# A state space recurrence in two levels, and cache pages requested in two of three units

## The chip, the cores and the metric

The kernel runs on one core of a Trainium2 chip. The metric is the device time of one execution in microseconds, as the median of several runs. Five engines work side by side, each on its own queue in program order: TensorE (PE, with its weight loads as PEld), VectorE (DVE), ScalarE (ACT), GpSimd (POOL), and SyncE (SP), which here only issues DMA transfers.

## The reference

One layer of a hybrid decoder for 512 prompt tokens and 8 x 4 sample tokens (544 columns). The normalized input goes through one wide projection and then into three branches: causal pooling, sparse attention over a paged cache, and a complex diagonal state space. Each is gated, projected and merged, and one output projection follows. Two pieces matter here:

```python
# compression: each block of 64 cached tokens is projected to one key and one value
kc = jnp.einsum('bnlkd,lde->bnke', blk[:, :, :, 0] + pe_cmp[0][:, None, :], w_phi[0])
vc = jnp.einsum('bnlkd,lde->bnke', blk[:, :, :, 1] + pe_cmp[1][:, None, :], w_phi[1])
# state space: h[s] = a * h[s-1] + bu[s], complex, for 64 groups x 64 states
_, _, hr, hi = lax.associative_scan(_complex_affine_combine, (a_re, a_im, bu_re, bu_im), axis=1)
```

## The kernel before

**Units.** The weights lie in blocks of 128 x 1024 (`wd`), one per unit. `M_LIST` gives the order of the projection's output tiles, `UNITS` one entry per weight block, and the loop at the end of `tile_hybrid_kernel` walks through them with `step`. In `in_unit` a unit is one half of the columns (272) of one output tile over all 16 blocks of rows. Every product is done three times by `mm3` (L149 to L151), with a high and a low half of each operand, so a unit has 48 matmuls of 272 columns. A pool unit (`pool_unit`) has 24. Units take the PSUM tiles `d` (three buffers) in turn.

**A step.** `step` writes out by hand what is queued for a unit: deferred functions (mostly stores, put off with `later` by one step), one `next` for each background generator in `bg`, the evacuation of the unit before (`pend_evac`), the split of the weights two units ahead (`w_split`: ScalarE rounds to `whi`, L144, and `lo_eng[0]` subtracts to get `wlo`, L145), the next weight load (`w_load`, L133, three raw buffers, so it waits until a split has freed one), and then the unit's matmuls. With `early[0]` set, the split and the load stand ahead of the generators. All loads and stores are issued on SP, in this order.

**The background.** `main_bg` runs beside the projection: `g_compress`, `g_ssm`, `g_compress_prompt`, `g_prompt`, `g_decode` one after the other; each `yield` ends its share of a step. `g_params` runs beside `g_compress` and prepares the constants of the state space on VectorE (L690 and following), from an input `par` that it loads itself.

**Compression.** `g_compress` has 16 jobs (8 sequences x 2 halves), each with 16 pages of 128 KB in a tile `ca` (two buffers), and takes three units for a job: 5, 5 and 6 of the 16 steps of d, two matmuls each (L620). Each matmul reads all 16 pages. In each of the three units `fetch` asks for a part of the next job's pages: SP reads the page numbers (L583) and issues one DMA per page (L587).

**State space.** `g_ssm` works on chunks of 8 tokens: 64 chunks for the prompt. Matmuls give the contribution of each chunk to the state at its end, copied to `SH` [128, 2 (real, imaginary), 32, 73]: columns 0 to 7 are the samples' states, 8 is zero, 9 to 72 the 64 chunks. The recurrence then goes over the chunks one after the other (L885 to L897): SH[c+1] += A8 * SH[c], complex, as four VectorE operations on [128, 2, 32] (two products, their sum, the addition), six chunks per step. `A8` is the coefficient of 8 tokens. While it runs, `lo_eng[0]` is GpSimd, so that L145 leaves VectorE. Then come the sample states (L904 to L907), the store of them and of the last prompt state (`hp`), two steps' ends, and the outputs: tiles `T` and `bd` are cleared by GpSimd, `make_u` (L935 to L941) builds factors on VectorE and GpSimd, and the first matmuls of the next step (L1006) read them. The pools `wk_s`, `rk_s` and `yk_s` follow each other in the same memory; `sq` lives through `g_ssm`.

Of the kernel before, what the change touches and what calls it, by code (L numbers as in the profile page):

```python
# [10 lines left out]
F32 = mybir.dt.float32  # L11
# [3 lines left out]
OP = mybir.AluOpType  # L15
# [51 lines left out]
def kernel(ctx, tc, a):  # L67
    nc = tc.nc
    pe, dve, act, pool, sp = nc.tensor, nc.vector, nc.scalar, nc.gpsimd, nc.sync
# [5 lines left out]
    def R(name, bufs=1):  # L75
        return tc.tile_pool(name=name, bufs=bufs, side="right")
# [9 lines left out]
    def bank(tag, bufs):  # L86
        return psb.tile([128, 512], F32, name=tag, tag=tag, bufs=bufs)
# [33 lines left out]
    lo_eng = [dve]  # L121
# [33 lines left out]
    def later(fn):  # L155
        deferred.append(fn)
# [425 lines left out]
    def gather(dsts, table, col):  # L582
        _, regs = nc.values_load_multi_w_load_instructions(  # L583
            PT[0:1, col:col + len(dsts)], engines=[mybir.EngineType.SP], min_val=0, max_val=NPOOL - 1,
            skip_runtime_bounds_check_because="the page table is clamped on the chip after its load")
        for dst, r in zip(dsts, regs):
            sp.dma_start(dst, a[table].rearrange("(g p) x -> g p x", p=128)[bass.ds(r, 1)]  # L587
                         .rearrange("g p x -> (g p) x"))

    def g_compress():  # L590
        with ExitStack() as s:
            cp = s.enter_context(R("cmp"))
            wphi = cp.tile([128, 2, 32, 64], F32, name="wphi")
            sp.dma_start(wphi, a["wphi"])
            ca_s = ExitStack()
            cap = ca_s.enter_context(R("ca", 2))
            jobs = [(b, h) for b in range(8) for h in range(2)]
            tiles = {}

            def fetch(n, pages):  # L600
                if n >= len(jobs):
                    return
                b, h = jobs[n]
                if n not in tiles:
                    tiles[n] = cap.tile([128, 16, 256], F32, name="ca")
                gather([tiles[n][:, pg, :] for pg in pages], f"c{h}", b * 16 + pages[0])
            for pg in range(0, 16, 4):
                fetch(0, range(pg, pg + 4))
                yield
            acc_b = None  # L610
            for n, (b, h) in enumerate(jobs):
                t = tiles.pop(n).rearrange("q g (k e j) -> q g k e j", k=2, j=8)
                if h == 0:
                    acc_b = bank("s", 2)
                for d0, d1, pgs in ((0, 5, (0, 6)), (5, 10, (6, 11)), (10, 16, (11, 16))):
                    fetch(n + 1, range(*pgs))
                    for d in range(d0, d1):
                        dd = h * 16 + d
                        for k in range(2):
                            pe.matmul(acc_b[k * 64:(k + 1) * 64, :128], lhsT=wphi[:, k, dd, :],  # L620
                                      rhs=t[:, :, k, d, :], start=(dd == 0), stop=(dd == 31))
                    yield
                if h:
                    act.activation(KC[:, b, :], acc_b[:, :128], AF.Copy)
            yield
            ca_s.close()
        done.add("cache")
# [171 lines left out]
    def g_ssm():  # L799
        while not {("su", 7), "params"} <= done:  # L800
            yield
        AR, BB, CC, A8 = (SSM[n] for n in ("AR", "BB", "CC", "A8"))
        s = ExitStack()
        sq = s.enter_context(R("ssm"))
        SH = sq.tile([128, 2, 32, 73], F32, name="sh")
# [42 lines left out]
        for n in range(10):  # L848
            i = n - 2
# [5 lines left out]
            i = n - 1  # L855
# [26 lines left out]
        rk_s = ExitStack()  # L882
        rp = rk_s.enter_context(R("ssmr", 2))
        m = dve.tensor_tensor
        lo_eng[0] = pool  # L885
        for c0 in range(0, 64, 6):
            for c in range(c0, min(64, c0 + 6)):
                prev = SH[:, :, :, 8 + c]
                nxt = SH[:, :, :, 9 + c]
                t1_ = rp.tile([128, 2, 32], F32, name="t1")  # L890
                t2_ = rp.tile([128, 2, 32], F32, name="t2")
                m(t1_, A8[:, 0], prev, op=OP.mult)  # L892
                m(t2_, A8[:, 1], prev[:, ::-1], op=OP.mult)  # L893
                m(t1_, t1_, t2_, op=OP.add)  # L894
                m(nxt, nxt, t1_, op=OP.add)  # L895
            yield
        lo_eng[0] = dve  # L897
        t1_ = rp.tile([128, 2, 32, 8], F32, name="h41", bufs=1)
        t2_ = rp.tile([128, 2, 32, 8], F32, name="h42", bufs=1)
        h0v = SH[:, :, :, 0:8]  # L900
# [5 lines left out]
            m(t1_[:, r_], t1_[:, r_], t2_[:, r_], op=OP.subtract if r_ == 0 else OP.add)  # L906
        m(S2, S2, t1_, op=OP.add)  # L907
        later(lambda: sp.dma_start(a["ssms"], S2))
        hp = rp.tile([128, 2, 32], F32, name="hp", bufs=1)
        pool.tensor_copy(hp, SH[:, :, :, 72])  # L910
        later(lambda: sp.dma_start(a["ssmp"], hp))
        yield
        yield
        rk_s.close()
        yk_s = ExitStack()
# [55 lines left out]
        for n in range(11):  # L971
            i = n - 3
# [11 lines left out]
            i = n - 2  # L984
# [8 lines left out]
            i = n - 1  # L993
# [6 lines left out]
            i = n  # L1000
# [623 lines left out]
    def main_bg():  # L1624
        yield from g_compress()
        early[0] = True
        yield from g_ssm()
        early[0] = False
        yield from g_compress_prompt()
        yield from g_prompt()  # L1630
        yield from g_decode()
        early[0] = True
        att_s.close()
        open_y()
        yield from prep_y(0, ypool, "pz")
        yield from prep_z()
# [4 lines left out]
    for u in range(4, len(UNITS)):  # L1641
# [6 lines left out]
        if un[0] == "in":  # L1648
            kind, i = M_LIST[un[1]]
# [166 lines left out]
    for u in range(first_tail, len(UNITS)):  # L1816
# [9 lines left out]
        else:  # L1826
# [4 lines left out]
            m, half = un[1:] if un[1] < 14 else ((14, 0), (15, 0), (14, 1), (15, 1))[u - len(UNITS) + 4]  # L1831
# [174 lines left out]
```

## Time and profile before

| | |
|---|---|
| median of 3 runs | 2327.85 us (2323.11 to 2331.73) |
| the profiled execution | 2324.99 us, span 2323.2 us |
| TensorE busy | 2243.1 us (97%), 19478 matmuls |
| TensorE weight loads busy | 2150.7 us (93%) |
| VectorE busy | 1110.6 us (48%) |
| ScalarE, GpSimd busy | 653.3 us (28%), 163.9 us (7%) |
| mean DMA rate | 154 GB/s |
| mean granted TensorE clock | 0.986 |

Times in the rows are microseconds from the start of the span. A busy TensorE is not TensorE at its peak, since matmuls are pipelined; so its waits and the number of matmuls in a stretch say more than its busy share. [...] The compression runs from about 75 to 451 us, the recurrence from 547 to 639.

### The profile page before, as it was taken

Reading aid. Unit: us, or ns where it says so; the run is one execution under the profiler, and the core shown is the slowest. Engines: PE = TensorE matmul, PEld = TensorE weight load, DVE = VectorE, ACT = ScalarE, POOL = GpSimd, SP = SyncE. Lnnn points to the kernel's source line nnn. Section 1 sums busy time; section 2 is a strip of 40 time slices with the busy share of each in tenths; the row PEclk is TensorE's granted clock in tenths of the full one; section 3 lists DMA queues with packets and bytes.
Section 4 is the critical chain, followed back from the end, with each engine's and each line's share of the span. In section 5 each row is a group of like instructions: output and inputs, shape, how many; then the busy total and the mean of one; then the engine's idle time right before and its main releaser. Section 6 shows DMA issues by size and latency. Waiting matters only on the chain.

```text
span 2323.2 us, 47074 instructions
## 1 busy us (share of the span) xinstructions
PE 2243.1 (97%) x19478; PEld 2150.7 (93%) x19478; DVE 1110.6 (48%) x2157; ACT 653.3 (28%) x1113; POOL 163.9 (7%) x132
## 2 busy tenths in 40 slices
PE   8999899999899999999999999999999999999995
PEld 8988799998889999999999998789999999999995
DVE  6234552256963246666665343323444536453225
ACT  5111111131022114444444222222332222222231
POOL 2000000142261000000000000000000002100003
PEclk9999999999999999999999999999999999999998
DMA  6766667562245655233222668875543645343333
GB/s 233 207 177 159 169 193 203 148 141 82 80 129 140 208 188 173 84 96 116 90 85 74 185 197 253 273 255 162 158 131 129 209 157 199 133 136 102 116 99 97
DMA packets 297128, 358.25 MB, mean 154 GB/s; under 512 B 137169, under 2 KB 219730, under 8 KB 296530
## 3 DMA queue, kind: packets, MB, share of 16 engines
q1 hardware_dynamic: 296914, 355.23, 50.3%
q8 instruction: 154, 2.52, 0.4%
q14 instruction: 60, 0.49, 0.1%
HBM read 309.33 MB, written 54.13 MB: 156 GB/s over the span
## 4 chain that ended last, share of the span: by engine, by line
PE 78%; DVE 5%; SPq 1%; DMA 1%; issue 1%; POOL 0%; ACT 0%; DVEq 0%; POOLq 0%; ACTq 0%
PE d L149 23%; PE d L151 22%; PE d L150 22%; PE o L1234 2%; PE s L1170 2%; PE t L1210 2%; PE s L620 1%; DVE t L892 1%; SPq L587 1%; DVE t L893 1%; DVE t L894 1%; PE s L953 1%; DVE sh L895 1%; PE o L1514 1%; PE s L1431 1%
## 5 line engine op out<-in xcount | busy, mean ns | idle before, releaser
L149 PE MATMUL d<-xh,whi 128*128 128x272 f32 x3424 | 1012.6, 296 | 20.5 <-DVE e L324 14.4
L151 PE MATMUL d<-xl,whi 128*128 128x272 f32 x3424 | 989.6, 289 | 0.0
L150 PE MATMUL d<-xh,wlo 128*128 128x272 f32 x3424 | 988.8, 289 | 0.0
L149 PEld LDWEIGHTS d<-xh,whi 128*128 128x128 f32 x3424 | 650.3, 190 | 47.4 <-issue 30.9
L151 PEld LDWEIGHTS d<-xl,whi 128*128 128x128 f32 x3424 | 649.8, 190 | 0.8 <-DVE xl L232 0.6
L150 PEld LDWEIGHTS d<-xh,wlo 128*128 128x128 f32 x3424 | 650.4, 190 | 0.0
L145 DVE TENSOR_TENSOR wlo<-wr,whi 128x1024 fp32r<-128x1024 f32 x298 | 378.1, 1270 | 300.8 <-ACT whi L144 298.3
L144 ACT ACTIVATE whi<-wr 128x1024 fp32r<-128x1024 f32 x309 | 323.0, 1052 | 474.9 <-PE d L151 376.4
L324 DVE TENSOR_TENSOR e<-d,rstd 128x272 f32<-128x272 f32 x186 | 81.7, 439 | 410.7 <-PE d L151 397.6
L149 PE MATMUL d<-mh,whi 128*128 128x272 f32 x512 | 148.4, 290 | 0.0
L151 PE MATMUL d<-ylA,whi 128*128 128x272 f32 x512 | 147.6, 288 | 0.0
L149 PE MATMUL d<-yhA,whi 128*128 128x272 f32 x512 | 147.5, 288 | 0.0
L150 PE MATMUL d<-yhA,wlo 128*128 128x272 f32 x512 | 147.4, 288 | 0.0
L151 PE MATMUL d<-ml,whi 128*128 128x272 f32 x512 | 147.4, 288 | 0.0
L150 PE MATMUL d<-mh,wlo 128*128 128x272 f32 x512 | 147.1, 287 | 0.0
L151 PE MATMUL d<-ylB,whi 128*128 128x272 f32 (+2 forms) x384 | 110.8, 289 | 0.0
L150 PE MATMUL d<-yhB,wlo 128*128 128x272 f32 (+2 forms) x384 | 110.8, 288 | 0.0
L149 PE MATMUL d<-yhB,whi 128*128 128x272 f32 (+2 forms) x384 | 110.6, 288 | 0.0
L149 PEld LDWEIGHTS d<-mh,whi 128*128 128x128 f32 x512 | 96.4, 188 | 0.0
L151 PEld LDWEIGHTS d<-ylA,whi 128*128 128x128 f32 x512 | 96.4, 188 | 0.0
L150 PEld LDWEIGHTS d<-yhA,wlo 128*128 128x128 f32 x512 | 96.3, 188 | 0.0
L151 PEld LDWEIGHTS d<-ml,whi 128*128 128x128 f32 x512 | 96.3, 188 | 0.0
(386 smaller groups left out, 2528.4 us busy)
## 6 DMA issues: line engine op xcount, KB each, us to landing
wr<-wd SPq DMA_DIRECT2D x309, 512.0 KB, 3.9
ca<-c SPq DMA_DIRECT2D x256, 128.0 KB, 3.3
gk<-ck SPq DMA_DIRECT2D x128, 128.0 KB, 2.2
gv<-cv SPq DMA_DIRECT2D x128, 128.0 KB, 3.3
gates<-e SPq DMA_DIRECT2D x48, 272.0 KB, 4.4
lg<-gates SPq DMA_DIRECT2D x48, 272.0 KB, 4.0
xo<-xT SPq DMA_DIRECT2D x32, 136.0 KB, 3.5
yT<-yo SPq DMA_DIRECT2D x32, 136.0 KB, 1.8
```

Of the source, the lines that this page charges most:

```text
L144: act.activation(hi, r, AF.Copy)
L145: lo_eng[0].tensor_tensor(lo, r, hi.bitcast(F32), op=OP.subtract)
L149: pe.matmul(ps, lhsT=h, rhs=xh, start=start, stop=False)
L150: pe.matmul(ps, lhsT=l, rhs=xh, start=False, stop=False)
L151: pe.matmul(ps, lhsT=h, rhs=xl, start=False, stop=stop)
L324: dve.tensor_tensor(out[:, cols(hf)], ps[:, :HALF], rstd[:, cols(hf)], op=OP.mult)
L587: sp.dma_start(dst, a[table].rearrange("(g p) x -> g p x", p=128)[bass.ds(r, 1)] .rearrange("g p x -> (g p) x"))
L620: pe.matmul(acc_b[k * 64:(k + 1) * 64, :128], lhsT=wphi[:, k, dd, :], rhs=t[:, :, k, d, :], start=(dd == 0), stop=(dd == 31))
L892: m(t1_, A8[:, 0], prev, op=OP.mult)
L1170: pe.matmul(st[n][k][:, off:off + nk], lhsT=QS[pg][k][:, qt * 128:(qt + 1) * 128], rhs=KS[br, k][j][:, :nk], start=(j == 0), stop=(j == 1))
L1210: pe.transpose(b[:, c:c + 128], st[n][k][:, c:c + 128], ident)
L1234: pe.matmul(o[hs[k], qt * 128:(qt + 1) * 128], lhsT=VN[:, kb, br, pg // 4, hs[k]], rhs=st[n][k][:, off + kb * 128:off + (kb + 1) * 128], s ...
```

## The change

Compression: the 16 pages of the next job are asked for in the first two of its three units, eight in each; none in the third. Recurrence: the 64 chunks become 8 blocks (k) of 8 chunks (j). First the powers 1 to 8 of the coefficient are made (`PP`, and `PS_` with the sign for the imaginary part). Then all blocks advance together over their own chunks (seven advances of 8 columns), the last chunks of the blocks advance one after the other (seven of one column), and each chunk j of blocks 1 to 7 gets the end of the block before, times the power j + 1 (seven of 7 columns). An advance has four operations as before. The columns lie 8 elements apart in `SH`. `lo_eng[0]` stays VectorE. `hp` moves from the pool `rp` to `sq`. The number of steps between the first step of the recurrence and the one that clears `T` stays 13.

```diff
--- before.py
+++ after.py
@@ -612,8 +612,9 @@
                 t = tiles.pop(n).rearrange("q g (k e j) -> q g k e j", k=2, j=8)
                 if h == 0:
                     acc_b = bank("s", 2)
-                for d0, d1, pgs in ((0, 5, (0, 6)), (5, 10, (6, 11)), (10, 16, (11, 16))):
-                    fetch(n + 1, range(*pgs))
+                for d0, d1, pgs in ((0, 5, (0, 8)), (5, 10, (8, 16)), (10, 16, ())):
+                    if pgs:
+                        fetch(n + 1, range(*pgs))
                     for d in range(d0, d1):
                         dd = h * 16 + d
                         for k in range(2):
@@ -882,19 +883,48 @@
         rk_s = ExitStack()
         rp = rk_s.enter_context(R("ssmr", 2))
         m = dve.tensor_tensor
-        lo_eng[0] = pool
-        for c0 in range(0, 64, 6):
-            for c in range(c0, min(64, c0 + 6)):
-                prev = SH[:, :, :, 8 + c]
-                nxt = SH[:, :, :, 9 + c]
-                t1_ = rp.tile([128, 2, 32], F32, name="t1")
-                t2_ = rp.tile([128, 2, 32], F32, name="t2")
-                m(t1_, A8[:, 0], prev, op=OP.mult)
-                m(t2_, A8[:, 1], prev[:, ::-1], op=OP.mult)
-                m(t1_, t1_, t2_, op=OP.add)
-                m(nxt, nxt, t1_, op=OP.add)
-            yield
-        lo_eng[0] = dve
+        PP = rp.tile([128, 2, 32, 8], F32, name="pp8", bufs=1)
+        PS_ = rp.tile([128, 2, 32, 8], F32, name="ps8", bufs=1)
+
+        def tmps(n):
+            return [rp.tile([128, 2, 32, 8], F32, name=f"t{i}")[:, :, :, :n] for i in (1, 2)]
+
+        dve.tensor_copy(PP[:, 0, :, 0], A8[:, 0, 0])
+        dve.tensor_copy(PP[:, 1, :, 0], A8[:, 1, 1])
+        for n in (1, 2, 4):
+            xr_, xi_ = PP[:, 0, :, 0:n], PP[:, 1, :, 0:n]
+            wr_, wi_ = (PP[:, r_, :, n - 1:n].to_broadcast([128, 32, n]) for r_ in range(2))
+            t1_, t2_ = tmps(n)
+            m(t1_[:, 0], xr_, wr_, op=OP.mult)
+            m(t1_[:, 1], xi_, wi_, op=OP.mult)
+            m(t2_[:, 0], xr_, wi_, op=OP.mult)
+            m(t2_[:, 1], xi_, wr_, op=OP.mult)
+            m(PP[:, 0, :, n:2 * n], t1_[:, 0], t1_[:, 1], op=OP.subtract)
+            m(PP[:, 1, :, n:2 * n], t2_[:, 0], t2_[:, 1], op=OP.add)
+        dve.tensor_scalar(PS_[:, 0], PP[:, 1], -1.0, None, op0=OP.mult)
+        dve.tensor_copy(PS_[:, 1], PP[:, 1])
+        yield
+        V = SH[:, :, :, 9:73].rearrange("q r g (k j) -> q r g k j", j=8)
+
+        def advance(dst, src, e, n):
+            t1_, t2_ = tmps(n)
+            m(t1_, PP[:, 0:1, :, e:e + 1].to_broadcast([128, 2, 32, n]), src, op=OP.mult)
+            m(t2_, PS_[:, :, :, e:e + 1].to_broadcast([128, 2, 32, n]), src[:, ::-1], op=OP.mult)
+            m(t1_, t1_, t2_, op=OP.add)
+            m(dst, dst, t1_, op=OP.add)
+
+        for j in range(1, 8):
+            advance(V[:, :, :, :, j], V[:, :, :, :, j - 1], 0, 8)
+            if j in (1, 3, 4, 6, 7):
+                yield
+        for k in range(1, 8):
+            advance(V[:, :, :, k:k + 1, 7], V[:, :, :, k - 1:k, 7], 7, 1)
+            if k in (4, 7):
+                yield
+        for j in range(7):
+            advance(V[:, :, :, 1:8, j], V[:, :, :, 0:7, 7], j, 7)
+            if j in (1, 3, 5, 6):
+                yield
         t1_ = rp.tile([128, 2, 32, 8], F32, name="h41", bufs=1)
         t2_ = rp.tile([128, 2, 32, 8], F32, name="h42", bufs=1)
         h0v = SH[:, :, :, 0:8]
@@ -906,10 +936,9 @@
             m(t1_[:, r_], t1_[:, r_], t2_[:, r_], op=OP.subtract if r_ == 0 else OP.add)
         m(S2, S2, t1_, op=OP.add)
         later(lambda: sp.dma_start(a["ssms"], S2))
-        hp = rp.tile([128, 2, 32], F32, name="hp", bufs=1)
+        hp = sq.tile([128, 2, 32], F32, name="hp")
         pool.tensor_copy(hp, SH[:, :, :, 72])
         later(lambda: sp.dma_start(a["ssmp"], hp))
-        yield
         yield
         rk_s.close()
         yk_s = ExitStack()
```

## Rows read from the trace of the kernel before

**Rows 1.** The chain that ended last, by engine (the page, part 4)

```profile
PE 78%; DVE 5%; SPq 1%; DMA 1%; issue 1%; POOL 0%; ACT 0%; DVEq 0%; POOLq 0%; ACTq 0%
```

**Rows 2.** TensorE's waits, 140 to 345 us: us in total, times, longest

```profile
PE s L620 <- DMA ca<-c: 21.7, 6, 7.2
```

**Rows 3.** Stretches: length, engines' busy time (instructions), clock, DMA share, GB/s

```profile
...
283.10:290.20 7.10, 0.00 (x0) 0.00 (x0) 1.73 (x2) 1.06 (x1) 0.00 (x0) 0.78 0.59 142
314.90:317.20 2.30, 0.00 (x0) 0.00 (x0) 2.09 (x8) 1.26 (x2) 0.00 (x0) 1.00 0.73 188
sum 21.20, PE 0.00 PEld 0.00 DVE 11.11 ACT 3.37 POOL 0.00; mean PE 0.00 PEld 0.00 DVE 1.85 ACT 0.56 POOL 0.00
```

**Rows 4.** The same view, stretches of 10 us; first in each, PE

```profile
170.00:180.00 10.00, 10.00 (x79) 9.35 (x75) 1.22 (x4) 0.00 (x0) 0.00 (x0) 0.78 0.68 228
...
320.00:330.00 10.00, 10.00 (x86) 9.68 (x85) 7.51 (x36) 0.00 (x0) 0.00 (x0) 0.94 0.41 81
...
550.00:560.00 10.00, 10.00 (x83) 10.00 (x81) 9.41 (x27) 1.35 (x2) 3.41 (x2) 1.00 0.27 83
```

**Rows 5.** The same view, the recurrence and an undisturbed part of the compression

```profile
546.90:657.73 110.83, 91.59 (x680) 90.15 (x678) 102.79 (x288) 15.84 (x16) 35.63 (x20) 0.93 0.27 88
350.00:450.00 100.00, 100.00 (x927) 95.63 (x928) 20.61 (x28) 17.30 (x22) 0.00 (x0) 1.00 0.62 181
```

**Rows 6.** SP in order of time: start, us, line, transfer, count

```profile
271.33 2.40 SPq L587 DMA_DIRECT2D ca<-c  x5
...
282.42 2.42 SPq L587 DMA_DIRECT2D ca<-c  x5
...
316.32 7.20 SPq L395 DMA_DIRECT2D gsc<-e  x12
```

**Rows 7.** VectorE in order of time; in brackets idle before, releaser

```profile
304.13 0.18 DVE L690 TENSOR_SCALAR v<-par 128x32 f32<-128x32 f32 x1 [18.70 <-DMA par<-spar]
...
307.45 0.43 DVE L324 TENSOR_TENSOR e<-d,rstd 128x272 f32<-128x272 f32 x1
...
309.55 1.22 DVE L145 TENSOR_TENSOR wlo<-wr,whi 128x1024 fp32r<-128x1024 f32 x1 [0.51 <-ACT whi L144]
```

**Rows 8.** Transfers issued from 150 to 345 us: count, size, us to landing

```profile
ca<-c SPq DMA_DIRECT2D x128, 128.0 KB, 4.4
```

**Rows 9.** The chain in order of time: start, us

```profile
342.15 1.31 PE s L620 x20
```

**Rows 10.** TensorE's waits, 546 to 660 us: us in total, times, longest

```profile
PE d L149 <- DVE e L324: 14.4, 6, 4.7
PE t L1006 <- POOL bd L941: 4.8, 1, 4.8
```

**Rows 11.** Operations of a tile or line: shortest/median/longest ns, first and last start

```profile
L892 DVE TENSOR_TENSOR t<-a,sh x64: 261/280/2374, 546.9 to 637.7; 128x64 f32<-128x64 f32 x64
...
L895 DVE TENSOR_TENSOR sh<-sh,t x64: 272/281/291, 547.7 to 638.5; 128x64 f32<-128x64 f32 x64
...
L894 DVE TENSOR_TENSOR t<-t,t x64: 224/226/2299, 547.4 to 638.2; 128x64 f32<-128x64 f32 x64
```

**Rows 12.** Groups by form: count | busy us, mean ns | idle before

```profile
L1750 DVE TENSOR_SCALAR e<-e 128x512 f32<-128x512 f32 x8 | 5.5, 689 | 0.3
...
L907 DVE TENSOR_TENSOR s<-s,h 128x512 f32<-128x512 f32 x1 | 0.7, 691 | 0.0
...
L788 DVE TENSOR_SCALAR cc<-cc 128x512 f32<-128x512 f32 x1 | 0.4, 419 | 0.0
...
L145 POOL TENSOR_TENSOR wlo<-wr,whi 128x1024 fp32r<-128x1024 f32 x11 | 26.9, 2442 | 101.0 <-ACT whi L144 101.0
```

**Rows 13.** The recurrence's end in order of time: VectorE, GpSimd, TensorE

```profile
645.04 0.69 DVE L907 TENSOR_TENSOR s<-s,h 128x512 f32<-128x512 f32 x1
...
649.21 0.96 POOL L918 MEMSET T<- 128x1024 f32 x1 [5.28 <-DMA ssmp<-hp]
...
657.73 1.08 PE L1006 MATMUL t<-u,bd 128*32 128x128 f32 x16 [4.85 <-POOL bd L941]
```

## The prediction

> **What bounds the kernel now.** I read the chain of waits first: TensorE's own lines carry nearly all of it [rows 1], so only what leaves TensorE waiting, or slows its clock, is worth anything. Then I asked who TensorE waits for in the two places that the diff touches.
>
> In the compression of the page cache it waits six times for pages, 21.7 us together [rows 2]. Cut out one by one, these stretches are empty on TensorE: 7.1 us at 283, 2.3 at 315, and 11.8 in the four before them, 21.2 in all [rows 3]. Each lies in front of the first matmul of a new job, whose last five pages SP asked for only one unit before. At 282.42 SP starts to issue the five pages that TensorE needs at 282.8; the fetch before had been issued at 271.33 [rows 6]. In between SP stood at the weight load, which waits for VectorE to free a raw buffer.
>
> In the recurrence TensorE waits 14.4 us for VectorE's evacuations and once 4.8 us for GpSimd [rows 10]. Here VectorE is the bound: it is busy 102.8 of 110.8 us, and TensorE does 680 matmuls in a stretch [rows 5] in which the undisturbed pace, 83 in 10 us [rows 4], would need 81.9. So 28.9 us are lost in it: 19.2 in the waits, the rest mostly at the lower clock level that follows them.
>
> **The pages.** The same 16 loads per job are issued in two units instead of three, so the last ones start a unit (about 7.4 us) earlier, and no fetch stands in the third. The price is on SP's queue: a page takes about 0.5 us to issue (five in 2.42 [rows 6]), so a weight load behind eight pages is issued 1 to 1.5 us later than behind five or six. It is used three units after its issue, and that hides it. If that cover were gone, TensorE would wait those 1.5 us in two units of three, 32 times, and the gain would be gone too. The four early stretches then close: eight pages started about 11 us before they are needed land 4.4 us [rows 8] after the last issue. [...] Early part: 11.8 + 2.6 = **14.4 us**.
>
> The late two (7.1 + 2.3, and 1.8 of clock, 11.2 us) I don't count in full, for something else is late next. VectorE's parameter chain waits until 304.13 for its input, and only then come an evacuation and the low halves of the weights, done at 310.77 [rows 7]. SP has 16 pages in front of that input before (5 + 6 + 5) and after (8 + 8), so it lands no more than some 2 us earlier. TensorE, no longer held at 283, would be done with its units at about 305 and wait for those low halves. Behind the same VectorE step stand twelve small DMAs, 7.2 us on SP from 316.32 [rows 6], and then the next job's pages: eight from about 324.6, eight from 330, the last issued at 334.2 and landed 4.4 us later, at 338.6. That unit began at 342.15 [rows 9]. So 3.5 us are kept, up to 5.5 with the earlier input; I take **4.5**. Bounds of the whole part: 11.8 (waits of the early four alone) to 25.6 (all).
>
> **The recurrence.** Removed: 256 VectorE operations of 64 elements, and 11 low halves on GpSimd. Those held VectorE up: one takes 2.44 us [rows 12], and an operation of the recurrence that meets it takes up to 2374 ns instead of 280 [rows 11]. Added on VectorE, in twelve steps up to the last advance:
> - the powers of the coefficient: 18 small operations of about 0.25 us (between 226 and 280 ns [rows 11]) and four copies: 5.4 us;
> - seven advances of 512 elements, each with three operations whose state operand lies 32 bytes apart, and one plain addition; seven more of 448 elements; seven of 64 elements, at 1.07 us each as now (280 + 280 + 226 + 281).
> - eleven low halves at 1.22 us (13.4) and eleven evacuations at 0.43 (4.7) [rows 7].
>
> A plain 512-element operation takes 691 ns [rows 12]. For the spaced ones the trace has two answers. L892 and L895 touch the same tile with one element per 292 bytes and take 280 and 281 ns, where L894, whose tiles are dense, takes 226 [rows 11]: 54 ns for 64 elements, 0.84 ns each, and no more when both source and result are spaced. That gives 1.12 us for 512 and 1.00 for 448 (plain 0.62). Against it stands L1750, which writes 512 elements 32 bytes apart in 689 ns [rows 12]: no dearer than the plain addition, though dearer than a dense operation of its own kind, L788, 419 ns [rows 12]. I take 0.84 because L892 and L895 are the same kind of operation on the same tile. Then: 7 x (3 x 1.12 + 0.69) = 28.4, 7 x (3 x 1.00 + 0.62) = 25.3, 7 x 1.07 = 7.5, with the powers 66.6 us. Without the surcharge it is 49.6; with it twice over where source and result are both spaced (14 operations) 72.2.
>
> [...]
>
> From 546.9: 66.6 + 13.4 + 4.7 = 84.7, so the last advance ends at 631.6. An evacuation, a gate operation, a low half (together 2.4) and the sample states (six operations of 256 elements, about 0.42 between 226 ns for 64 and 691 for 512, and one of 0.69: 3.2 us) follow: 637.2, against 645.04 + 0.69 = 645.7 now [rows 13]. Now GpSimd starts to clear T 3.5 us after that, since T takes over the memory of hp, which is being stored [rows 13]; with hp in the longer-lived pool this wait goes. The store itself comes a step later and nobody waits for it. GpSimd's work up to TensorE's first K matmul takes 657.73 - 649.21 = 8.5 us: 645.7 instead of 657.73, a gain of **12.0 us**. TensorE could be there by 629 (657.73 - 28.9), so it still waits, for VectorE and then GpSimd. The generator takes 13 steps from first recurrence step to T, before and after, so everything behind it stays in the same units. Bounds: without the surcharge VectorE needs 67.7 us up to the last advance where TensorE needs 12 x 48 matmuls, 69.4 us: TensorE is the bound, all 28.9 come back. With the double one 12.0 - 5.6 = 6.4.
>
> **The sum.** 14.4 + 4.5 + 12.0 = 30.9 us off the profiled execution of 2325.0: **2294 us**. That execution lies 2.9 us under the median of the three runs and inside their range, so I leave it there.
>
> **Rivals.**
> 1. Spaced operands cost nothing (L1750 is right). VectorE keeps up, the recurrence gives 28.9: 2325.0 - 18.9 - 28.9 = 2277. For it: L1750 has the exact spacing. Against: L892 and L895. Chance 0.22.
> 2. The pages don't pay: eight in a row on SP and the DMA engines make the weights late, or a wait on VectorE's low halves takes the place of each page wait. Only the recurrence gives: 2325.0 - 12.0 = 2313. For it: SP does stand at the weight load behind VectorE, and at 305 I expect such a wait myself. Against: TensorE's list of waits in that stretch has almost nothing but pages [rows 2]. Chance 0.14; about 0.09 of it within 0.5%.
> 3. Slower: spaced operations at 32 bytes cost far more than at 292. There are 42. The whole gain of 30.9 is used up at 0.74 us more each, about 1.8 us on average instead of 1.06; at 2.4 us each the recurrence ends 56 us later, 2294 + 56 = 2350. For it: nothing in the trace shows a long operation of two tensors with this spacing. Against: L895 reads and writes spaced elements and pays 55 ns for 64; L1750. Chance 0.04.
>
> **How the numbers follow.** My forecast has 0.60. The range joins the bounds: 2325.0 - 11.8 - 6.4 = 2307 and 2325.0 - 25.6 - 28.9 = 2271 (rounded up and down); rival 1 lies inside, about 2 in 10 outside. A measurement of this kernel can tell 0.5%, 11.6 us, from no change. Faster by more: 0.60 + 0.22 + 0.05 = 0.87; within: 0.09; slower: 0.04.
>
> **What would show it.** Right: no wait for pages between 160 and 265, one of a few us near 305 for low halves or near 335 for pages; spaced operations of 512 near 1.1 us; GpSimd's wait for the store of hp gone; TensorE still waiting some us for evacuations and for GpSimd. Wrong: spaced operations near 0.69 us and no wait for VectorE (rival 1); TensorE waiting for weights in the first two units of each job (rival 2); spaced operations above 1.8 us (rival 3).

## The result and the profile after

The changed kernel takes 2303.77 us (median of 4 runs, 2303.46 to 2305.63) against 2327.39 us before (4 runs, 2323.11 to 2331.73): a ratio of 0.990, interval 0.988 to 0.992. That is 23.6 us less, where the sum had 30.9 and, from the median, 33. Between the two profiled executions it is 21.2 us of span (2323.2 and 2302.0). The direction was right and the time lies in the range, so the question is which term was too large.

The page of the changed kernel (span 2302.0 us): the engines' busy time, and the chain that ended last by engine.

```profile
PE 2237.1 (97%) x19478; PEld 2145.1 (93%) x19478; DVE 1105.2 (48%) x2018; ACT 652.6 (28%) x1113; POOL 137.9 (6%) x121
...
PE 79%; DVE 5%; DMA 2%; issue 1%; SPq 1%; ACT 0%; POOL 0%; DVEq 0%; ACTq 0%; POOLq 0%
```

Beside [rows 1] nothing moves here: TensorE still carries the chain. What moved is seen only stage by stage. TensorE's waits from 140 to 345 us (total, times, longest), as [rows 2]:

```profile
PE s L621 <- DMA ca<-c: 4.1, 1, 4.1
PE d L149 <- ACT whi L144: 4.0, 2, 3.1
PE d L150 <- DVE wlo L145: 2.7, 2, 1.8
PE o L398 <- DVE e L390: 2.1, 1, 2.1
...
```

Of the 21.7 us of waits for pages 4.1 are left, but 8.8 us of waits for ScalarE and VectorE have come, and 1.1 in two smaller ones. For the recurrence, its waits from 500 to 660 us and its whole stretch, as [rows 10] and [rows 5]:

```profile
PE t L1035 <- POOL bd L970: 6.2, 1, 6.2
PE d L149 <- DVE e L324: 4.9, 4, 2.4
```

```profile
538.40:636.67 98.27, 87.15 (x678) 86.12 (x676) 93.22 (x146) 15.73 (x16) 8.38 (x9) 0.98 0.30 99
```

98.3 us for 678 matmuls at a granted clock (a share of full speed) of 0.98, where it was 110.8 for 680 at 0.93.

To set the two parts apart I use two landmarks that every kernel here has: the start of ScalarE's last copy of the chunks' contributions (before the recurrence) and TensorE's first K matmul (behind it). Up to the first, all that was gained came from the pages; between the two, all from the recurrence. Starts in us, the last column being the difference:

| kernel | last copy | ahead of before | first K matmul | copy to matmul |
|---|---|---|---|---|
| before | 535.69 | | 657.73 | 122.0 |
| after | 527.16 | 8.5 | 636.67 | 109.5 |
| pages alone | 528.80 | 6.9 | 650.96 | 122.2 |
| recurrence alone | 539.51 | -3.8 | 648.98 | 109.5 |
| small load a step or two earlier | 518.51 | 17.2 | 627.98 | 109.5 |
| small load ahead of the pages | 520.82 | 14.9 | 630.35 | 109.5 |
| dense working copy | 529.55 | 6.1 | 627.35 | 97.8 |
| low halves on GpSimd | 525.79 | 9.9 | 644.34 | 118.6 |
| dense copy and small load earlier | 522.12 | 13.6 | 619.93 | 97.8 |

The recurrence gained 12.5 us (the sum had 12.0). The pages gained 8.5 (it had 18.9, and 11.8 as the least). The recurrence alone has the same code as before ahead of its copy, yet its copy starts 3.8 us later: a single execution of the page part scatters by about that much, the recurrence by about a tenth of a microsecond.

Not all of a lead at these landmarks reaches the end. From the first K matmul to the end of the span the kernels take 1665.1 to 1671.4 us, partly because TensorE waits longer there for loads of cached keys: 4.9 us in the changed kernel, 7.3 with the small load a step or two earlier, 8.9 with it ahead of the pages. With the small load a step or two earlier, a lead over the changed kernel of 8.7 us at the copy is 5.9 us of span, and 5.3 us between the medians.

### The profile page after: what moved, and what is told of

Same layout as the page of the kernel before. It is cut to its first block, busy times and chain, and to the rows that moved or that the text cites. A ratio compares the mean times of both kernels' runs of the same rounds, so it can differ in the third digit from the quotient of the medians.

```text
span 2302.0 us, 46935 instructions
## 1 busy us (share of the span) xinstructions
PE 2237.1 (97%) x19478; PEld 2145.1 (93%) x19478; DVE 1105.2 (48%) x2018; ACT 652.6 (28%) x1113; POOL 137.9 (6%) x121
## 3 DMA queue, kind: packets, MB, share of 16 engines
HBM read 309.33 MB, written 54.13 MB: 158 GB/s over the span
## 4 chain that ended last, share of the span: by engine, by line
PE 79%; DVE 5%; DMA 2%; issue 1%; SPq 1%; ACT 0%; POOL 0%; DVEq 0%; ACTq 0%; POOLq 0%
PE d L149 23%; PE d L151 22%; PE d L150 22%; PE o L1263 2%; PE t L1239 2%; PE s L1199 2%; PE s L621 1%; PE s L982 1%; PE o L1543 1%; DVE wlo L145 1%; PE s L1460 1%; DVE t L911 1%; DVE t L912 1%; SPq L587 1%; PE s L993 1%
## 5 line engine op out<-in xcount | busy, mean ns | idle before, releaser
L145 DVE TENSOR_TENSOR wlo<-wr,whi 128x1024 fp32r<-128x1024 f32 x309 | 393.1, 1273 | 300.7 <-ACT whi L144 296.9
L324 DVE TENSOR_TENSOR e<-d,rstd 128x272 f32<-128x272 f32 x186 | 81.7, 439 | 408.9 <-PE d L151 386.3
L151 PE MATMUL d<-ylB,whi 128*128 128x272 f32 (+2 forms) x384 | 110.8, 288 | 0.0
L150 PE MATMUL d<-yhB,wlo 128*128 128x272 f32 (+2 forms) x384 | 110.8, 288 | 0.0
```

Of the source, the lines that this page charges most:

```text
L145: lo_eng[0].tensor_tensor(lo, r, hi.bitcast(F32), op=OP.subtract)
L150: pe.matmul(ps, lhsT=l, rhs=xh, start=False, stop=False)
L151: pe.matmul(ps, lhsT=h, rhs=xl, start=False, stop=stop)
L324: dve.tensor_tensor(out[:, cols(hf)], ps[:, :HALF], rstd[:, cols(hf)], op=OP.mult)
```

## Where the pages' gain went

Stretches of 40 us in the compression: length, busy time and count of TensorE, weight loads, VectorE, ScalarE, GpSimd, then granted clock, DMA share, GB/s. First before, then after.

```profile
160.00:200.00 40.00, 32.88 (x279) 31.30 (x279) 13.87 (x31) 5.51 (x10) 0.00 (x0) 0.91 0.64 166
200.00:240.00 40.00, 37.06 (x333) 35.25 (x333) 18.21 (x40) 6.77 (x12) 0.00 (x0) 0.96 0.65 173
240.00:280.00 40.00, 37.97 (x362) 36.01 (x361) 21.29 (x46) 7.39 (x11) 0.00 (x0) 1.00 0.73 176
```

```profile
160.00:200.00 40.00, 40.00 (x388) 38.08 (x390) 20.24 (x41) 7.65 (x11) 0.00 (x0) 1.00 0.76 183
200.00:240.00 40.00, 38.04 (x338) 35.95 (x335) 19.36 (x40) 6.69 (x11) 0.00 (x0) 0.96 0.68 170
240.00:280.00 40.00, 36.06 (x323) 34.18 (x322) 19.18 (x42) 6.52 (x10) 0.00 (x0) 0.96 0.78 193
```

From 160 to 200 us the forecast comes true at once: 109 matmuls more and a full clock. From 240 to 280 TensorE does 39 fewer than before. So something is late there that was not late before. The same place in order of time (start, us; in brackets idle before, releaser), SyncE, VectorE, ScalarE, TensorE of the changed kernel:

```profile
256.17 5.95 SPq L587 DMA_DIRECT2D ca<-c  x8
263.23 0.61 SPq L462 DMA_DIRECT2D pe_s<-poolT  x1
...
266.79 0.31 DVE L484 TENSOR_TENSOR pcA<-pe_s 128x144 f32<-128x144 f32 x1 [5.54 <-DMA pe_s<-poolT]
...
270.27 0.63 ACT L494 ACTIVATE pdh<-psA 128x512 fp32r<-128x512 f32 x1 [17.22 <-DVE psA L489]
270.92 1.99 ACT L144 ACTIVATE whi<-wr 128x1024 fp32r<-128x1024 f32 x2
...
272.02 0.39 PE L149 MATMUL d<-pdh,whi 128*128 128x272 f32 x1 [3.07 <-ACT whi L144]
```

`pe_s` is the state of the causal pooling: 60 KB for each of eight tiles (0 to 7), asked for when the first half of the tile is evacuated, and read by VectorE one step later. When a pool unit follows, its matmuls stand in that same step, behind what VectorE makes of the load. The load's issue stands on SP behind the page requests of the same step. These were six or five pages; now they are eight, issued in 5.95 us. The same place before:

```profile
263.92 3.77 SPq L587 DMA_DIRECT2D ca<-c  x6
268.11 0.62 SPq L462 DMA_DIRECT2D pe_s<-poolT  x1
...
273.14 0.31 DVE L484 TENSOR_TENSOR pcA<-pe_s 128x144 f32<-128x144 f32 x1 [0.94 <-DMA pe_s<-poolT]
```

In the changed kernel VectorE would have been free for it at 261.25 (266.79 - 5.54), two microseconds before SP issued it at 263.23. The pooled sum then goes to ScalarE (L494), the split of the next weights stands behind that in ScalarE's order, and TensorE waits 3.07 us for the split and 0.87 for the low halves. A wait "for the weights' high half" is thus one for a 60 KB load at the far end of this chain, as the runs with an earlier load show below; the list of waits alone names the wrong suspect.

## Experiments

Times are medians; ratios are to the kernel before in the same series of runs (2328.86 us for the first four, 2329.39 us for the other four).

**Pages alone, recurrence alone.** Do the two parts add up, and which is short? Pages alone is the kernel before with

```diff
-for d0, d1, pgs in ((0, 5, (0, 6)), (5, 10, (6, 11)), (10, 16, (11, 16))):
-    fetch(n + 1, range(*pgs))
+for d0, d1, pgs in ((0, 5, (0, 8)), (5, 10, (8, 16)), (10, 16, ())):
+    if pgs:
+        fetch(n + 1, range(*pgs))
```

> The pages in two of three units, with the recurrence of before. The changed kernel's trace shows weight split number 48 (at 342 us) 8.5 us earlier than before. If the two parts simply add, this kernel gives that alone: 2327.4 - 8.5 = 2319 us (2316 to 2322). If the recurrence only gained because the compression left more room, or the other way round, it differs from that by more than 4 us. Both theories of the missing page gain (the small load of the pooling state behind eight pages; or VectorE's pooling chain, late by itself) expect the same here: waits of TensorE in front of two pool units, near 230 and 269 us.

and recurrence alone is the changed kernel with these lines as they were.

> The recurrence in two levels, with the pages asked for in three units as before. If the parts add: 2327.4 - 12.7 = 2315 us (2312 to 2318), the six page waits as before (21.7 us) and TensorE's waits for evacuations near 5 us instead of 14.4, for GpSimd near 6 us.

Pages alone: 2320.3 us (2315.05 to 2323.94), ratio 0.996 (0.995 to 0.998). Recurrence alone: 2318.15 us (2316.08 to 2318.42), ratio 0.996 (0.994 to 0.997); this is 3 us more than expected and just outside the range given. Its six waits in front of new jobs are there as before, 21.9 us. The product of the ratios is 0.992, at the edge of the interval of both together (0.988 to 0.992). So they add about up, and the table of landmarks says the same: 122.2 and 109.5 us between the landmarks, with and without the new recurrence. Pages alone has the stall of the changed kernel in the place of the page waits; from 140 to 345 us:

```profile
PE d L149 <- ACT whi L144: 4.1, 2, 2.3
PE s L621 <- DMA wr<-wd: 4.1, 1, 4.1
...
```

The second row is the late wait in front of the job at 333.68. Its matmuls read pages and nothing of `wd`, so the load named is only the one that landed last.

The shortfall thus belongs to the page part, not to an interplay of the two.

**The small load a step or two earlier.** If the small load behind eight pages is the cause (theory A), asking for it earlier, at the head of a step, gives the lost gain back; if the pool units are held by something else (B), nothing changes.

```diff
+def load_es(i):
+    ES[i] = sub["pp"].tile([128, 8, 19], F32, name="pe_s", bufs=3)
+    sp.dma_start(ES[i][:, :, 0:15], a["poolT"][i])
...
-es = st["es"] = pp.tile([128, 8, 19], F32, name="pe_s")
-sp.dma_start(es[:, :, 0:15], a["poolT"][i])
+if i == 0:
+    load_es(0)
+es = st["es"] = ES.pop(i)
+if i < 7:
+    later(lambda: load_es(i + 1))
```

The load is asked for one step earlier than in the changed kernel, and two steps earlier for tiles 3, 5 and 7, because a pool unit is carried out between the halves of tiles 2, 4 and 6.

> The changed kernel, with the small load of the pooling state (60 KB) asked for a tile ahead and at the head of a step, in front of the pages, instead of behind them. Theory A (that load lands late because it stands behind eight pages, and VectorE and with it ScalarE's weight split wait): VectorE's waits for it (11.6 us in four) go, TensorE's waits in front of the pool units near 230 and 269 us (2.4 and 4.6 us, with the low clock behind them) go, and the time is 2303.8 - 7 = 2297 us (2295 to 2299). Theory B (with the page waits gone, the pooling chain on VectorE is too long by itself): the waits stay above 5 us together, and the time stays at 2302 to 2305.

2298.51 us (2297.33 to 2300.55), ratio 0.987 (0.986 to 0.989). All of TensorE's waits from 140 to 345 us, and the stretch from 240 to 280:

```profile
PE s L630 <- DMA ca<-c: 4.0, 1, 4.0
PE o L398 <- DVE e L390: 3.6, 1, 3.6
```

```profile
...
240.00:280.00 40.00, 40.00 (x375) 38.23 (x372) 19.03 (x41) 6.53 (x10) 0.00 (x0) 1.00 0.90 214
```

The waits for ScalarE's and VectorE's halves are gone, TensorE is busy without a break from 240 to 280 us, with 375 matmuls instead of 323, and the granted clock stays at 1.00. At the last copy this kernel is 17.2 us ahead, 8.7 more than the changed kernel, where the sum had 18.9; that is more than twice the scatter, and the median says the same with 5.3 us. Theory A holds: the load was the cause.

**The small load ahead of the pages.** A load that starts earlier could also help by its time alone, whatever its place. Here it is asked for one step later than in the kernel before this one, again at a step's head. For tiles 1, 2, 4 and 6 that is the step of the changed kernel, so that only its place in front of the pages is new. For 3, 5 and 7 it is still one step earlier than there; the text put on record takes the step to be the same for all. The edit, against the kernel before this one:

```diff
-    later(lambda: load_es(i + 1))
+    later(lambda: later(lambda: load_es(i + 1)))
```

> The small load of the pooling state asked for in the same step as in the changed kernel, but at its head, in front of the eight pages instead of behind them. If its place behind the pages is the cause, VectorE's waits for it (11.6 us in four) fall below 3 us and the time is that of the kernel that asks a tile ahead, 2298.5 us (2296 to 2301). If it is only late because it is asked for one unit before its use, the waits stay above 8 us and the time is 2302 to 2305.

2299.71 us (2294.25 to 2303.72), ratio 0.987 (0.985 to 0.989). From 140 to 345 us:

```profile
PE s L630 <- DMA wr<-wd: 5.4, 2, 4.3
PE o L398 <- DVE e L390: 2.6, 1, 2.6
...
```

No wait for the small load is left, and 14.9 us are gained at the last copy, as much as with the earlier load within the scatter. Tile 7 on SP in order of time:

```profile
247.15 0.59 SPq L460 DMA_DIRECT2D pe_s<-poolT  x1
...
253.43 7.83 SPq L596 DMA_DIRECT2D ca<-c  x8
```

In the changed kernel this load (263.23) stood behind its step's pages (256.17); here it goes out a step before them. Of that kernel's four waits for the load (11.6 us), those for tiles 1 and 6 (1.29 and 0.65 us) went by the new place alone. The long ones, for tiles 5 and 7 (4.11 and 5.54 us), went with the new place and a step more, and no run here separates the two. An estimate from the changed kernel's rows says that the place would have been enough: from the load's issue to VectorE's first use of it there were 4.8 us for tile 5 (222.27 to 227.05) and 3.6 for tile 7 (263.23 to 266.79). Issued when its step's pages started, at 215.68 and 256.17, and with 4.8 us for both, it would have been there at 220.5 and 261.0, and VectorE was free at 222.94 and 261.25. So the late issue was the cause, and the pages ahead of it explain it by this estimate.

**A dense working copy.** Was VectorE's price for spaced operands still the limit of the recurrence (theory C), or was the rest of it TensorE's own or GpSimd's (D)? ScalarE puts the contributions into a tile in which the eight blocks of one chunk lie side by side; only the last level writes the spaced tile, and two ScalarE copies bring over the rest. The tile `A8`, which nothing reads any more, goes with its four operations.

```diff
+VD = vd_s.enter_context(R("ssmv")).tile([128, 2, 32, 8, 8], F32, name="vd")
...
-    advance(V[:, :, :, :, j], V[:, :, :, :, j - 1], 0, 8)
+    advance(VD[:, :, :, j, :], VD[:, :, :, j - 1, :], 0, 8)
...
-    advance(V[:, :, :, 1:8, j], V[:, :, :, 0:7, 7], j, 7)
+    advance(VD[:, :, :, j, 1:8], VD[:, :, :, 7, 0:7], j, 7, V[:, :, :, 1:8, j])
```

> The changed kernel, with the states of the prompt copied by ScalarE to a tile in which the columns of one operation lie side by side; the last addition of the third level writes back to the spaced places, ScalarE copies what it doesn't touch. Same arithmetic. Theory C (the spacing of the operands is what makes VectorE late): operations of 512 fall from 1.17 to about 0.69 us, VectorE saves some 17 us, TensorE's waits for evacuations (4.9 us) go and that for GpSimd (6.2 us) falls by 4 or more: 2303.8 - 10 = 2294 us (2290 to 2296). Theory D (the time goes with the number of operations and the low halves, whatever the spacing): operations stay above 1 us or the waits stay, and the time is within 2302 to 2306.

2294.86 us (2292.87 to 2298.84), ratio 0.985 (0.984 to 0.987). Operations by form from 541 to 615 us (count, busy us, mean ns, idle before), and the recurrence's waits:

```profile
L911 DVE TENSOR_TENSOR sh<-vd,t 128x448 f32<-128x448 f32 x7 | 7.3, 1045 | 0.2
...
L911 DVE TENSOR_TENSOR vd<-vd,t 128x512 f32<-128x512 f32 x7 | 4.8, 692 | 0.2
```

```profile
PE t L1035 <- DVE u L966: 1.8, 1, 1.8
PE t L1035 <- POOL bd L970: 1.7, 1, 1.7
```

The dense operations take 0.69 us instead of 1.17 to 1.19 (below), the only spaced ones left (448 elements, spaced in the result alone) still 1.05. The waits for evacuations are gone, and the landmarks stand 97.8 us apart, 24.2 less than before and 11.7 less than in the changed kernel. Theory C holds.

**Low halves back on GpSimd.** The change left them on VectorE. Does that pay (E), or would a free VectorE gain more (F)?

```diff
+lo_eng[0] = pool
 PP = rp.tile([128, 2, 32, 8], F32, name="pp8", bufs=1)
...
+lo_eng[0] = dve
```

> The changed kernel, with the low halves of the weights on GpSimd during the recurrence, as before. Theory E (GpSimd's low half, 2.44 us, and a VectorE operation with two inputs in SBUF hold each other up): VectorE is rid of 12 low halves (14.6 us) but is held up about 2.2 us by each (26 us), so TensorE comes out of the recurrence about 10 us later: 2314 us (2308 to 2318). Theory F (relief): VectorE has 14.6 us less to do, TensorE's waits for evacuations go: 2303.8 - 8 = 2296 us (2293 to 2299).

2313.03 us (2310.34 to 2318.48), ratio 0.994 (0.992 to 0.996): 9 us of the recurrence's gain are lost. By form, 500 to 650 us:

```profile
L145 POOL TENSOR_TENSOR wlo<-wr,whi 128x1024 fp32r<-128x1024 f32 x12 | 38.8, 3246 | 87.3 <-ACT whi L144 87.2
...
L914 DVE TENSOR_TENSOR t<-t,t 128x512 f32<-128x512 f32 x7 | 11.1, 1584 | 0.2
```

One by one, from this kernel in order of time, the same operation once alone and once beside GpSimd:

```profile
545.41 0.69 DVE L914 TENSOR_TENSOR t<-t,t 128x512 f32<-128x512 f32 x1
...
549.84 2.80 DVE L914 TENSOR_TENSOR t<-t,t 128x512 f32<-128x512 f32 x1
```

GpSimd takes 1.22 us a piece off VectorE and costs it more than that: an addition that meets it takes 2.80 us instead of 0.69. GpSimd itself takes 3.25 us, where it took 2.44 beside the small operations [rows 12]. The evacuation L324, which reads one of its inputs from PSUM, was not held up: in the trace of before the one at 592.62 us takes 0.43 us inside one of GpSimd's low halves (592.44 to 594.91), as it does alone, and L892 right behind it, with both inputs in SBUF, 2.07 us instead of 0.28. So leaving the low halves on VectorE is a part of the gain.

**What the spacing costs.** The prediction had two contradicting answers, L892 and L895 against L1750. A bench was put into the changed kernel behind the compression: 256 elements each, with operands side by side, 8, 16 and 32 bytes apart: additions (L641 to L644 with one input, L646 with the result, L647 with one input and the result, L648 with all three spaced) and products with a constant (L650 dense, L651 with the result spaced, L652 with the input spaced). The operations, without what stands between them:

```diff
+tt(BD_, B2[:, 0:256], BT, op=OP.add)
+tt(BD_, B2[:, 0:512:2], BT, op=OP.add)
+tt(BD_, B2[:, 0:1024:4], BT, op=OP.add)
+tt(BD_, BI[:, :, 0], BT, op=OP.add)
...
+tt(BO[:, :, 0], B2[:, 0:256], BT, op=OP.add)
+tt(BO[:, :, 0], BI[:, :, 0], BT, op=OP.add)
+tt(BO[:, :, 0], BI[:, :, 0], BI[:, :, 4], op=OP.add)
...
+dve.tensor_scalar(BD_, B2[:, 0:256], 0.5, None, op0=OP.mult)
+dve.tensor_scalar(BO[:, :, 0], B2[:, 0:256], 0.5, None, op0=OP.mult)
+dve.tensor_scalar(BD_, BI[:, :, 0], 0.5, None, op0=OP.mult)
```

> The price of a spaced operand by itself: behind the compression, with GpSimd idle, VectorE does additions of 256 elements, three times each, with one input dense, 8, 16 and 32 bytes apart, then with only the result 32 bytes apart, with one input and the result, with both inputs and the result; and a product with a constant dense, with a spaced result, with a spaced input. They stand beside the kernel's work, which they lengthen; its time means nothing. [...]

The rows of the bench's tile (shortest/median/longest ns, first and last start):

```profile
L641 DVE TENSOR_TENSOR bo<-bi,bt x3: 417/418/418, 463.5 to 500.5; 128x256 f32<-128x256 f32 x3
L642 DVE TENSOR_TENSOR bo<-bi,bt x3: 424/426/426, 463.9 to 500.9; 128x256 f32<-128x256 f32 x3
L643 DVE TENSOR_TENSOR bo<-bi,bt x3: 610/614/622, 464.4 to 501.4; 128x256 f32<-128x256 f32 x3
L644 DVE TENSOR_TENSOR bo<-bi,bt x3: 670/672/680, 465.0 to 502.1; 128x256 f32<-128x256 f32 x3
L646 DVE TENSOR_TENSOR bo<-bi,bt x3: 644/660/674, 469.5 to 506.5; 128x256 f32<-128x256 f32 x3
L647 DVE TENSOR_TENSOR bo<-bi,bt x3: 694/703/703, 470.2 to 507.2; 128x256 f32<-128x256 f32 x3
L648 DVE TENSOR_TENSOR bo<-bi x3: 700/709/710, 470.9 to 507.9; 128x256 f32<-128x256 f32 x3
L650 DVE TENSOR_SCALAR bo<-bi x3: 284/285/288, 475.5 to 512.5; 128x256 f32<-128x256 f32 x3
L651 DVE TENSOR_SCALAR bo<-bi x3: 426/431/449, 475.8 to 512.8; 128x256 f32<-128x256 f32 x3
L652 DVE TENSOR_SCALAR bo<-bi x3: 428/442/464, 476.3 to 513.3; 128x256 f32<-128x256 f32 x3
```

At 8 bytes apart an addition costs next to nothing more (426 ns against 418). At 16 it costs 0.77 ns an element ((614 - 418) / 256), at 32 bytes 0.99, and with all three operands spaced 1.14: it is paid about once, not once for each operand. So the step is between 8 bytes and 16. Why 32 bytes cost more than 16 (672 against 614) no row shows. The product with a constant is another kind: dense it is faster than an addition (285 against 418), spaced it falls back to 431 or 442, about the time of a dense addition. That is why L1750 seemed free: its 689 ns were compared with an addition's 691, and its own dense kind takes 419 at that size [rows 12].

**Both mends together.** The dense copy and the earlier small load in one kernel.

> Both mends together: the dense tile for the recurrence and the early load of the pooling state. They lie in different stages, so they should add: 2303.8 - 5.3 - 8.9 = 2290 us (2287 to 2294).

2284.08 us (2279.95 to 2290.08), ratio 0.9805 (0.979 to 0.982), below both kernels. The median came out 6 us under what was expected, and below the range given; the expected time lies at the upper end of the five runs, and the profiled one (2290.08) is the slowest of them. Why the others are faster is not settled. The longest wait left from 140 to 345 us:

```profile
PE o L398 <- DVE e L390: 7.5, 1, 7.5
...
```

That is the wait behind VectorE's parameter chain near 300 us, whose input stands behind the pages on SP. Moving that load, or the twelve small stores behind it, was not tried.

## Why the prediction was right, and where it was not

**The early page waits: the step that failed.** The cause of the waits was right: with pages a unit earlier they are gone, and from 160 to 200 us TensorE does 388 matmuls instead of 279. What failed is the sentence on the price on SP's queue. It looked at one thing behind eight pages, the weight load, which is used three units later, and that cover held: with the small load out of the way no wait of TensorE for a half of the weights is left. It did not list what else SP issues behind the pages: the small load of the pooling, used one unit later. Measured at the parameter chain's first operation (304.13 in [rows 7], 297.53 after), behind the early waits, the changed kernel is 6.6 us ahead, where 14.4 were forecast. With the small load a step or two earlier that operation starts at 287.91, 16.2 us ahead, so the term itself was sound. The lost part is almost all this load, within the scatter; 1.4 us of it is TensorE's wait in front of the first job (3.3 us after, 1.9 before). Pages alone, with the same code up to there, has 2.2, so that this is at least in part scatter.

The sum's 2.6 us for the slower clock behind the early four waits, and the 1.8 behind the late two, are an estimate from four stretches of before: beside the 79 and 86 matmuls of [rows 4], 82 from 220 to 230 us (granted clock 0.89) and 80 from 290 to 300 (0.81), where the pace of [rows 5] gives 92.7 in 10 us. No run shows these terms by themselves; the kernel with the small load a step or two earlier shows the waits and the slow clock gone together (1.00 from 160 to 280 us), and for both the 16.2 us.

The price of a page was also too low: 0.5 us came from five pages issued in 2.42 us [rows 6]. Eight took 5.95 in the row above, 0.74 each; at the same place before, six stood ahead of the small load and took 3.77, so it is 2.2 us later from the pages alone, not 1 to 1.5. The trace of before could have told: VectorE waited for this load there too, 3.7 us in three places (one is the row at 273.14 above), so it had no cover left.

Rival 2 had a piece of this, a wait that takes the place of a page wait. It named VectorE's low halves; the runs show the pooling's load, and at two of the four early places, not all.

**The late page waits: right in the waits, too much in the gain.** The two waits came where they were forecast: TensorE waited 1.8 us for low halves up to 309.33 and 4.2 us for pages up to 332.16. The job that began at 342.15 [rows 9] begins 10.0 us earlier, 3.4 more than the 6.6 ahead of it; with the small load earlier it begins at 322.43, 3.5 more than the 16.2. The sum had 4.5, and 3.5 as its lower end. What the sum left out is the lower clock behind the very wait that it forecast. In the first 10 us of that job the changed kernel does 84 matmuls at a granted clock of 0.84 (0.50 up to 335.3 us, 1.00 from there), and 70 at 0.72 with the small load earlier, where the kernel before does 99 at 1.00. So 1.5 and 2.5 us are lost again, 8.5 and 17.2 arrive at the recurrence, and the term of 4.5 was worth 1.9 in the changed kernel. Of the 10.4 us that the pages fell short, 7.8 are in the early term and 2.6 in this one.

**The recurrence: right, with small errors that cancel.** The operations by form, 500 to 650 us, as [rows 11, 12]:

```profile
L914 DVE TENSOR_TENSOR sh<-sh,t 128x512 f32<-128x512 f32 x7 | 8.3, 1191 | 0.2
L912 DVE TENSOR_TENSOR t<-ps,sh 128x512 f32<-128x512 f32 x7 | 8.2, 1172 | 0.0
L911 DVE TENSOR_TENSOR t<-pp,sh 128x512 f32<-128x512 f32 x7 | 8.2, 1169 | 0.1
L911 DVE TENSOR_TENSOR t<-pp,sh 128x448 f32<-128x448 f32 x7 | 7.2, 1034 | 0.0
...
L913 DVE TENSOR_TENSOR t<-t,t 128x512 f32<-128x512 f32 x7 | 4.8, 693 | 0.2
```

| term | forecast us | measured us |
|---|---|---|
| spaced operation of 512, of 448 | 1.12, 1.00 | 1.17 to 1.19, 1.03 |
| first operation to the sample states' end | 90.3 | 89.9 (538.40 to 628.26) |
| T cleared to the first K matmul | 8.5 | 8.3 (628.41 to 636.67) |
| gain of the recurrence | 12.0 | 12.5 |

The spaced operations of 512 cost 0.05 to 0.07 us more than taken (0.94 ns an element, (1177 - 693) / 512, against 0.84). That the stretch is no longer for it is seen in order of time: an operation starts before the one ahead of it has ended by its own row, so a sum of durations is a little too long. The powers gain most by it: 3.6 us (538.40 to 542.00) where 5.4 were taken. Against that stand 2.2 us of VectorE's waits for ScalarE in the stretch, which the sum had at nothing.

```profile
620.05 1.05 DVE L911 TENSOR_TENSOR t<-pp,sh 128x448 f32<-128x448 f32 x1
621.02 1.03 DVE L912 TENSOR_TENSOR t<-ps,sh 128x448 f32<-128x448 f32 x1
...
628.41 0.95 POOL L947 MEMSET T<- 128x1024 f32 x1 [37.15 <-DVE s L937]
```

The last row is GpSimd's clearing of T: it waits for the sample states and no longer for the store of `hp` [rows 13], as forecast. TensorE waits 4.9 us for evacuations and then 6.2 for GpSimd; the forecast had both waits, without a size.

**Rival 1** fell: no spaced operation of 512 came near 0.69 us. The dense copy, in which only seven additions are still spaced, shows about what it would have brought: 24.2 us, not 28.9, since 3.5 us of waits for VectorE's `u` and GpSimd's `bd` come next. **Rival 3** fell: 1.19 us is far from 1.8.

**Where the 2303.77 lies.** 2325.0 less 8.5 and 12.5 is 2304. The pages' 8.5 is below the 11.8 that the prediction took as the least for them. That the time is still within 2307 is luck for this part: the bound joins the least of both parts, and the recurrence gave 12.5 instead of its least, 6.4.

## What to carry to other kernels

When a change makes a block of transfers on a queue longer, list every transfer behind that block and ask of each when its reader needs it; here the small one with a near reader set the price, not the large one with a far reader. A cover shown for one of them says nothing about the others. And where two rows contradict each other on a price, first see whether they are of the same kind of operation: a row that is slow for its kind can look cheap beside another kind.

## What the runs showed of the hardware

- The time that SP takes to issue a row of page requests varies, and long rows vary most: five took 2.40 to 3.51 us and six 2.92 to 4.28 before, eight 3.96 to 8.31 in the changed kernel (60 to 345 us). So about 0.5 us a page is what five mostly took, and eight seldom. What SP waits for in them no row shows.
- VectorE's price for 4-byte elements that lie apart starts between 8 bytes (426 ns for 256 elements, 418 dense) and 16 (614). At 32 bytes it is paid about once for an operation, whichever operands are spaced: 660 (result), 672 (one input), 709 ns (all three).
- GpSimd beside large two-input operations on VectorE costs both: 2.80 us for an addition of 0.69, and 3.25 us for a subtraction that took 2.44 beside small ones.
